# The last gates of an encoder trunk: two products moved ahead of a sum of squares, first outputs scaled on other engines, and squares summed by TensorE

## The chip, the cores and the metric

The kernel runs on one core of one Trainium2 chip. A core has five engines that run side by side, each through its own instructions in order: TensorE (PE in the profile; its weight loads are PEld), VectorE (DVE), ScalarE (ACT), GpSimd (POOL) and SyncE (SP), which issues transfers. The metric is the device time of one execution in microseconds (us), of which several runs were taken; one more execution was profiled.

## What is computed

Two requests of 512 and 256 tokens (768 in all, 1024 features) go through a trunk of two layers. Cut to the part that matters here, the end of the second layer and the last norm:

```
x = x + square(relu(h @ mlp_w_up)) @ mlp_w_down
gate = sigmoid(rms_norm(x, norm_ple) @ ple_w_gate)
x = x + (p @ ple_w_proj) * gate
y = rms_norm(x, final_norm)
# rms_norm(x, g) = x * rsqrt(mean(x * x over the 1024 features) + 1e-6) * g
```

## The kernel before, in words

Features lie on the partitions: x is 8 blocks of 128 features by 768 tokens, the first sequence's 512 tokens and then the second's 256. A product in near-fp32 accuracy is made of three: high weight by high input, high by low, low by high. So one gate product for one feature block is 8 x 3 = 24 matmuls into one PSUM bank. A sum over the features (over the partitions) is a matmul with a block of ones, whose result is the sum on every partition.

`last_ple` (line 1842) is the end of the program. Each of its two sequences has its own last norm (`first` and `second`, of the class `Last`). Its parts are these:

- For the first sequence, a loop over the 8 feature blocks: `gated` loads the operand `pr` (the finished product `p @ ple_w_proj`, line 1715), multiplies the gate product by the norm's factor (`gt`, VectorE, line 1718), takes the sigmoid (ScalarE, 1719), multiplies (VectorE, 1689) and adds to x (VectorE, 1721). `first.square` squares the new block (ScalarE, 257) and adds it to an accumulator (VectorE, 258).
- Then the code is laid out by hand: inside `tc.manual_schedule` the order on ScalarE, TensorE and VectorE is the order in which the code is written. The accumulator is split in two parts (`ah` on ScalarE, `al` on VectorE, both line 105/106), the second sequence's gate products 0 and 1 are made, and two matmuls with ones sum `ah` and `al` (the first sum of squares, tile `ss`). Out of it come a logarithm, an exponential, a square and three VectorE steps, lines 315 to 330; the result is the first sequence's factor `rf`.
- For the second sequence, block m by block m: `gate_of(m)` is the gate product, the load of its `pr` (line 1872) and the multiplication `gt` (1874); `sigmoid` (1879); `added` multiplies by `pr` (1689) and adds to x (1882); `shifted` squares the block on ScalarE (1886, 1888) and writes `y`, the block times its gain (1909). The squares of blocks 0 to 4 are added up on VectorE (1890). Between these stand the first sequence's outputs, `stored`: one VectorE instruction each that multiplies x by gain and by `rf` (1902), and a transfer out (1903).
- At the end four matmul terms in plain fp32 with ones (1960) sum the accumulator and the squares of blocks 5, 6 and 7; then come the same steps to a factor, the multiplication of `y` (1971) and four transfers out (1972).

SyncE issues the transfers in the order of the program. One whose data isn't there yet holds up those behind it.

Of the kernel before, what the change touches and what calls it, by code (L numbers as in the profile page):

```python
# [11 lines left out]
F32 = mybir.dt.float32  # L12
F32R = mybir.dt.float32r
AF = mybir.ActivationFunctionType
ALU = mybir.AluOpType
# [3 lines left out]
P = 128  # L19
D = 1024  # L20
KB = D // P
# [7 lines left out]
CH = 1024  # L29
# [19 lines left out]
def trunk_kernel(ctx: ExitStack, tc: tile.TileContext, a: dict, out: bass.AP):  # L49
    nc = tc.nc  # L50
    act, dve, pe = nc.scalar, nc.vector, nc.tensor
# [30 lines left out]
    def gain(i, m):  # L82
        return vec[:, i * KB + m : i * KB + m + 1]
# [10 lines left out]
    ones32 = const.tile([P, P], F32, name="ones32")  # L94
# [32 lines left out]
    def bank(tag, name):  # L127
        pool = pair_of_banks if tag == "B" else psum
        return pool.tile([P, 512], F32, tag=tag, name=name, bufs=BANKS[tag])

    def fresh(name="mm", n=1, tag=None):

        nonlocal shift
        if tag is None:
            shift += 1
            tag = "ACAB"[shift % 4]
        return bank(tag, name) if n == 1 else [bank(tag, name) for _ in range(n)]
# [62 lines left out]
    more = None  # L200

    def slot(i, name, dt=F32R, n=T):

        return (slots if i < 32 else more).tile([P, n], dt, tag=f"S{i}", name=name)

    def big(name, dt=F32):

        nonlocal turn
        if more is None:
            return tmp.tile([P, T], dt, tag="t", name=name)  # L210
        turn += 1
        return tmp.tile([P, T], dt, tag=f"q{turn % 6}", name=name, bufs=1)
# [733 lines left out]
    more = ctx.enter_context(tc.tile_pool(name="more", bufs=1))  # L946
# [6 lines left out]
    def x(m, o=0, n=T):  # L953
        return pairs[m // 2][:, m % 2, o : o + n]
# [737 lines left out]
    def gate(w, xs, o, n):  # L1692
        ts = terms_of(w, [[t[:, o : o + n] for t in p] for p in xs])
        if n == T:
            gp = both("gate")
            for j in range(2):
                for i, (wh, wl, xh, xl) in enumerate(ts):
                    for wt, xt in ((wl, xh),) if j else ((wh, xh), (wh, xl)):
                        for t, b, e in pieces(gp):
                            matmul(  # L1700
                                t,
                                wt,
                                xt[:, b:e],
                                start=i == j == 0 and xt is xh,
                                stop=i == len(ts) - 1 and j == 1,
                            )
            return pieces(gp)
        gp = fresh("gate")
        group(gp, ts, n)
        return [(gp[:, :n], 0, n)]  # L1710
# [131 lines left out]
    def last_ple(norm, ws, gps, parts, _, prs, ys, finals):  # L1842

        s0, s1 = SEQS
        first, second = Last(0, s0, *finals[0]), Last(s0, s1, *finals[1])

        def product(fin, m):
            return gate(ws[m], norm.xs, fin.o, fin.n)

        def block(fin, m, gp=None):  # L1850
            return gated(1, m, gp or product(fin, m), r, fin.o, fin.n, fin, prs)

        gps.append(product(first, 2))
        r = norm.rstd(psum, norm.sum_squares(psum, parts=parts))
        for m in range(KB):
            xb = block(first, m, gps[m] if m < 3 else None)
            if m < KB - 1:
                first.square(m, xb)

        groups = ((0, 1), (1, 2), (3, 3), (6, 2))  # L1860
        ys = [slot(i, "y", F32).rearrange("p (m n) -> p m n", n=s1) for i in ys]
        y = {m: ys[m // 3][:, m % 3, :] for m in range(KB)}

        outs = []
        left = list(range(KB))
        adds, held = [], []

        def gate_of(m):

            [(ps, _, _)] = product(second, m)  # L1870
            pr = slot(prs[m % 3], "pr", F32)
            nc.sync.dma_start(pr[:, :s1], pj[1][m, :, s0:])
            t = big("gt")
            dve.tensor_tensor(t[:, :s1], ps, r[:, s0:], ALU.mult)
            return t, pr

        def sigmoid(gate):
            t = gate[0]
            second.gated = act.activation(t[:, :s1], t[:, :s1], AF.Sigmoid).ins

        def added(m, t, pr):
            dve.tensor_tensor(x(m, s0, s1), x(m, s0, s1), gate_times(pr, t, s1), ALU.add)

        def squared(m):
            if m == 0:
                return act.activation(second.acc, x(m, s0, s1), AF.Square)
            sq = second.temp("sq")
            act.activation(sq, x(m, s0, s1), AF.Square)
            if m < KB - 3:
                adds.append(lambda: dve.tensor_tensor(second.acc, second.acc, sq, ALU.add))  # L1890
            else:
                held.append(sq)

        def stored(n):

            for _ in range(n):
                i = left.pop(0)
                if i % 2 == 0:
                    tag = ("sum0", "sum1", "zhi", "zlo")[i // 2]
                    outs.append(more.tile([P, CH], F32, tag=tag, name="o", bufs=1))  # L1900
                o = outs[i // 2][:, i % 2 * s0 : i % 2 * s0 + s0]
                dve.scalar_tensor_tensor(o, x(i, 0, s0), gain(6, i), rf, ALU.mult, ALU.mult)
                nc.sync.dma_start(out[i, :, :s0], o)

        ET = mybir.EngineType
        def shifted(m):
            if m < KB - 1:
                squared(m)
                act.activation(y[m], x(m, s0, s1), AF.Copy, scale=gain(6, m))

        with tc.manual_schedule(engines={ET.Activation, ET.PE, ET.DVE}):
            first.last = first.gated
            first.table()
            first.square(KB - 1, xb)
            parts = first.acc_parts()
            gates = [gate_of(m) for m in range(2)]
            ss = first.sum_squares(psum, parts=parts)
            logs, newton, result = first.rstd_steps(psum, ss)
            logs()
            newton()  # L1920
            result()
            rf = first.r
            for m in range(2):
                sigmoid(gates[m])
            added(0, *gates[0])
            shifted(0)
            gates.append(gate_of(2))
            sigmoid(gates[2])
            added(1, *gates[1])
            shifted(1)  # L1930
            for m in range(2, KB - 2):
                if m > 2:
                    gates.append(gate_of(m))
                    sigmoid(gates[m])
                for _ in range(len(adds)):
                    adds.pop(0)()
                if m > 2:
                    stored((2, 1, 2)[m - 3])
                added(m, *gates[m])
                if m < KB - 3:  # L1940
                    shifted(m)
            gates.append(gate_of(KB - 2))
            sigmoid(gates[KB - 2])
            shifted(KB - 3)
            t, pr = gates[KB - 2]
            pr = gate_times(pr, t, s1)
            gates.append(gate_of(KB - 1))
            sigmoid(gates[KB - 1])
            dve.tensor_tensor(x(KB - 2, s0, s1), x(KB - 2, s0, s1), pr, ALU.add)
            shifted(KB - 2)  # L1950
            added(KB - 1, *gates[KB - 1])
            m = KB - 1
            second.last = second.gated
            second.table()
            sq = second.temp("sq")
            dve.tensor_tensor(sq, x(m, s0, s1), x(m, s0, s1), ALU.mult)
            ss = fresh("ss")[:, :s1]
            terms = [second.acc, *held, sq]
            for i, z in enumerate(terms):
                pe.matmul(ss, lhsT=ones32[:], rhs=z, start=i == 0, stop=i == len(terms) - 1)  # L1960
            stored(1)
            logs, newton, result = second.rstd_steps(psum, [(ss, 0, s1)])
            logs()
            act.activation(y[m], x(m, s0, s1), AF.Copy, scale=gain(6, m))
            stored(2)
            newton()
            result()
            rf = second.r
            for m, n in groups:
                yb = ys[m // 3][:, m % 3 : m % 3 + n, :]  # L1970
                dve.tensor_tensor(yb, yb, rf[:, None, :].broadcast_to([P, n, s1]), ALU.mult)
                nc.sync.dma_start(out[m : m + n, :, s0:].rearrange("m p t -> p m t"), yb)
# [213 lines left out]
    held = old[8:13]  # L2186
# [124 lines left out]
```

## Time and profile before

| what | us |
|---|---|
| three runs: median (lowest to highest) | 1590.61 (1590.45 to 1590.7) |
| the profiled execution, its own time | 1591.22 |
| its span in the trace | 1589.4 |
| TensorE busy in the span | 1543.9 |
| last gate product of the first sequence ends | 1547.3 from the start |
| last matmul of the second sequence's gate products ends | 1576.3 from the start |

The profiled execution's time is 1.8 us more than its span. Times within the trace are counted from the span's start. A timeline row gives start, duration, engine, line, operation, tiles and a count, and in brackets how long the engine had stood idle and what ended that; "x18" are 18 merged instructions. A windows row gives a stretch, its length, the busy time of PE, PEld, DVE, ACT and POOL (with instruction counts), the clock granted to TensorE (1.00 is full), the DMA engines' busy share and GB/s.

### The profile page before, as it was taken

The page shows a single profiled execution, that of the slowest core. Times are in us where ns is not written, and L with a number is a line of the kernel's source. Part 1 is how long each engine was busy: PE and PEld are TensorE (multiplying, and loading weights), DVE is VectorE, ACT ScalarE, POOL GpSimd, SP SyncE. Part 2 cuts the span into 40 slices and gives each one's busy share as a digit, 9 for nine tenths or more (in the row PEclk, how much of TensorE's full clock was granted, in tenths as well). Part 3 has the DMA queues.
Part 4 walks back from the last instruction along what each step waited for, and adds up shares of the span by engine and source line. Part 5 has one row for each costly group of instructions (what it writes and reads, how often), then busy time and mean ns, then how long its engine had stood idle before and what let it go on. Part 6 is the DMA issues. An engine that isn't in the chain of part 4 may idle for free.

```text
span 1589.4 us, 24597 instructions
## 1 busy us (share of the span) xinstructions
PE 1543.9 (97%) x9375; PEld 1489.7 (94%) x9375; DVE 1357.7 (85%) x2244; ACT 982.2 (62%) x1566; POOL 151.0 (9%) x172
## 2 busy tenths in 40 slices
PE   9999999999999999999989999999999999999996
PEld 7988889999999999999989999999999999999885
DVE  7599898898889889889898887869888988988986
ACT  7478766876566656667755344556656665665754
POOL 0211000011111111110000000000111111111000
PEclk9999999999999999999999999999999999999998
DMA  8854412445654644556522212122564554456522
GB/s 278 216 135 134 132 52 91 128 100 129 137 120 120 140 115 105 129 137 152 147 60 80 80 67 85 63 78 69 138 137 114 128 139 102 108 137 140 138 78 103
DMA packets 72694, 188.39 MB, mean 119 GB/s; under 512 B 8144, under 2 KB 26064, under 8 KB 72576
## 3 DMA queue, kind: packets, MB, share of 16 engines
q1 hardware_dynamic: 45440, 139.89, 28.3%
q0 software_dynamic: 27136, 46.93, 16.7%
q8 instruction: 73, 1.20, 0.3%
q14 instruction: 45, 0.37, 0.1%
HBM read 143.02 MB, written 10.48 MB: 97 GB/s over the span
## 4 chain that ended last, share of the span: by engine, by line
PE 61%; DVE 22%; ACT 10%; issue 4%; DMA 4%; SPq 0%; DVEq 0%; ACTq 0%
PE a L180 28%; PE mm L180 7%; PE b L180 6%; PE B L180 4%; PE C L180 4%; PE c L180 3%; PE d L180 2%; DVE t L424 2%; PE pt L847 1%; ACT y L1149 1%; PE gate L180 1%; PE p L180 1%; DVE act L463 1%; DVE pr L1689 1%; PE O L857 1%
## 5 line engine op out<-in xcount | busy, mean ns | idle before, releaser
L180 PE MATMUL a<-xs,whi 128*128 128x384 f32 x624 | 116.0, 329 | 11.2 <-DVE y L1389 9.9
L180 PEld LDWEIGHTS a<-xs,whi 128*128 128x128 f32 x624 | 102.5, 189 | 16.4 <-DVE y L1389 13.8
L180 PE MATMUL a<-t,zhi 128*128 128x384 f32 x568 | 109.5, 326 | 0.0
L180 PE MATMUL a<-t,whi 128*128 128x384 f32 x568 | 109.3, 326 | 0.0
L180 PE MATMUL b<-t,zhi 128*128 128x384 f32 x552 | 106.7, 326 | 0.3 <-DVE t L424 0.3
L180 PE MATMUL a<-act,whi 128*128 128x384 f32 x512 | 104.3, 326 | 0.0
L1475 POOL DMA_DIRECT2D x<-p x56 | 68.0, 1215 | 367.2 <-DVE x L1457 216.0
L504 ACT ACTIVATE whi<-sum 128x1024 fp32r<-128x1024 f32 x71 | 74.9, 1055 | 41.9 <-PE a L180 39.1
L532 DVE TENSOR_TENSOR wlo<-wraw,whi 128x1024 fp32r<-128x1024 f32 x74 | 90.1, 1218 | 10.9 <-ACT whi L504 10.9
L180 PEld LDWEIGHTS a<-t,whi 128*128 128x128 f32 x568 | 94.9, 189 | 0.6 <-ACT d L1565 0.6
L180 PEld LDWEIGHTS a<-t,zhi 128*128 128x128 f32 x568 | 95.1, 189 | 0.4 <-DVE t L424 0.4
L180 PEld LDWEIGHTS b<-t,zhi 128*128 128x128 f32 x552 | 92.3, 189 | 0.9 <-DVE t L424 0.9
L504 ACT ACTIVATE vhi<-wraw 128x512 fp32r<-128x512 f32 x71 | 44.4, 625 | 75.3 <-PE B L180 64.3
L504 ACT ACTIVATE zhi<-sum 128x1024 fp32r<-128x1024 f32 x71 | 74.8, 1054 | 22.2 <-DVE sum L480 22.2
L532 DVE TENSOR_TENSOR wlo<-sum,whi 128x1024 fp32r<-128x1024 f32 x71 | 86.5, 1218 | 2.2 <-ACT whi L504 2.2
L1457 DVE TENSOR_TENSOR x<-x,a 128x384 f32<-128x384 f32 x128 | 67.3, 549 | 23.6 <-PE a L180 11.8
L180 PEld LDWEIGHTS a<-act,whi 128*128 128x128 f32 x512 | 86.6, 189 | 0.3
L532 DVE TENSOR_TENSOR zlo<-sum,zhi 128x1024 fp32r<-128x1024 f32 x69 | 84.0, 1217 | 0.0
L504 ACT ACTIVATE whi<-wraw 128x1024 fp32r<-128x1024 f32 x76 | 79.4, 1045 | 1.9
L180 PE MATMUL mm<-xs_mix,whi 128*128 128x512 f32 (+1 forms) x320 | 77.3, 331 | 0.4 <-DVE pjs L610 0.4
L418 ACT ACTIVATE t<-y 128x768 fp32r<-128x768 f32 x64 | 52.3, 838 | 22.9 <-DVE y L409 17.3
L1457 DVE TENSOR_TENSOR x<-x,C 128x384 f32<-128x384 f32 x64 | 35.1, 553 | 35.3 <-PE C L180 29.2
(336 smaller groups left out, 4424.7 us busy)
## 6 DMA issues: line engine op xcount, KB each, us to landing
wraw<-in_up SPq DMA_DIRECT2D x64, 512.0 KB, 4.8
wraw<-in_down SPq DMA_DIRECT2D x64, 512.0 KB, 4.9
x<-p POOLq DMA_DIRECT2D x56, 384.0 KB, 6.4
wraw<-in_w_in SPq DMA_DIRECT2D x24, 512.0 KB, 3.5
vlo<-in_down POOLq DMA_DIRECT2D x32, 256.0 KB, 7.5
wraw<-in_gate SPq DMA_DIRECT2D x16, 512.0 KB, 4.1
vlo<-in_up POOLq DMA_DIRECT2D x28, 256.0 KB, 7.3
pj<-pjs SPq DMA_DIRECT2D x16, 384.0 KB, 2.8
```

The lines of the kernel that those rows point to most:

```text
L180: pe.matmul(ps, lhsT=w, rhs=rhs, **flags)
L418: act.activation(t[0][:], (self.q1, self.q2)[i][:], AF.Copy)
L424: dve.tensor_tensor(lo[:], (self.q1, self.q2)[i][:], hi[:].bitcast(F32), ALU.subtract)
L463: dve.tensor_tensor(lo[:], self.q2[:], hi[:].bitcast(F32), ALU.subtract)
L504: act.activation(hi[:], src, AF.Copy)
L532: dve.tensor_tensor(lo[:], src, hi[:].bitcast(F32), ALU.subtract)
L847: pe.transpose(pt[:, h * P : (h + 1) * P], lg[h // 2][:, h % 2, b * P : (b + 1) * P], ident[:],)
L857: pe.matmul(O[:], lhsT=v, rhs=ph[:], start=b == 0, stop=False)
L1149: act.activation(t[:], t[:], AF.Square)
L1457: dve.tensor_tensor(t[:, o : o + H], t[:, o : o + H], f, op)
L1475: nc.gpsimd.dma_start(pairs[2 * h + 1][:, :, o : o + H], q, accum_op=ALU.add)
L1689: dve.tensor_tensor(q, q, natural(t[:, o:e]), ALU.mult)
```

## The change

Four things change in `last_ple`, and nothing elsewhere.

1. The second sequence's gate products 2 and 3 are made ahead of the first sum of squares (kept in `made`) instead of one by one afterwards.
2. The first outputs are made in two steps: ScalarE writes x times gain into the output tile (`scaled`, blocks 0 to 3 in the loop over the first sequence, 4 to 7 after the split of the accumulator), and GpSimd multiplies by `rf` in place. `stored` now asks for two outputs at a time, the first two before block 2 of the second sequence is added.
3. The second sequence's squares are not added on VectorE any more. Each is a matmul term into one PSUM tile `ss2`; `summed` issues the terms that have been gathered.
4. The four transfers of first outputs stand elsewhere among the loads of `pr`.

```
+        def scaled(i):
+            if i % 2 == 0:
+                tag = ("sum0", "sum1", "zhi", "zlo")[i // 2]
+                outs.append(more.tile([P, CH], F32, tag=tag, name="o", bufs=1))
+            o = outs[i // 2][:, i % 2 * s0 : i % 2 * s0 + s0]
+            act.activation(o, x(i, 0, s0), AF.Copy, scale=gain(6, i))
...
             if m < KB - 1:
                 first.square(m, xb)
+            if m < KB // 2:
+                scaled(m)
...
-            [(ps, _, _)] = product(second, m)
+            [(ps, _, _)] = made.pop(m) if m in made else product(second, m)
...
         def squared(m):
-            if m == 0:
-                return act.activation(second.acc, x(m, s0, s1), AF.Square)
-            sq = second.temp("sq")
+            sq = second.acc if m == 0 else second.temp("sq")
             act.activation(sq, x(m, s0, s1), AF.Square)
-            if m < KB - 3:
-                adds.append(lambda: dve.tensor_tensor(second.acc, second.acc, sq, ALU.add))
-            else:
-                held.append(sq)
+            held.append(sq)
+
+        def summed(last=False):
+            for sq in held:
+                pe.matmul(ss2, lhsT=ones32[:], rhs=sq, start=not counted, stop=last and sq is held[-1])
+                counted.append(sq)
+            held.clear()
...
                 o = outs[i // 2][:, i % 2 * s0 : i % 2 * s0 + s0]
-                dve.scalar_tensor_tensor(o, x(i, 0, s0), gain(6, i), rf, ALU.mult, ALU.mult)
+                nc.gpsimd.tensor_tensor(o, o, rf, ALU.mult)
                 nc.sync.dma_start(out[i, :, :s0], o)
...
             parts = first.acc_parts()
+            for i in range(KB // 2, KB):
+                scaled(i)
             gates = [gate_of(m) for m in range(2)]
+            made.update((m, product(second, m)) for m in (2, 3))
             ss = first.sum_squares(psum, parts=parts)
...
             rf = first.r
+            ss2 = fresh("ss")[:, :s1]
...
             shifted(1)
+            stored(2)
             for m in range(2, KB - 2):
                 if m > 2:
                     gates.append(gate_of(m))
                     sigmoid(gates[m])
-                for _ in range(len(adds)):
-                    adds.pop(0)()
+                if m > 3:
+                    summed()
                 if m > 2:
-                    stored((2, 1, 2)[m - 3])
+                    stored(2)
                 added(m, *gates[m])
                 if m < KB - 3:
                     shifted(m)
...
-            ss = fresh("ss")[:, :s1]
-            terms = [second.acc, *held, sq]
-            for i, z in enumerate(terms):
-                pe.matmul(ss, lhsT=ones32[:], rhs=z, start=i == 0, stop=i == len(terms) - 1)
-            stored(1)
+            held.append(sq)
+            summed(True)
+            ss = ss2
             logs, newton, result = second.rstd_steps(psum, [(ss, 0, s1)])
             logs()
             act.activation(y[m], x(m, s0, s1), AF.Copy, scale=gain(6, m))
-            stored(2)
             newton()
```

On TensorE, at the very end of the program, this is the order before: `gate_16561` is the second sequence's gate product 7, `ss_16600` its sum of squares.

```order
L180 MATMUL gate_16561<-xs_ple1_15896,gwr_15908 128x64x2x2
L180 MATMUL gate_16561<-xs_ple1_15895,gwr_15910 128x64x2x2
L1960 MATMUL ss_16600<-acc_final512_16033,ones32_126 128x256
L1960 MATMUL ss_16600<-sq_16557,ones32_126 128x256
L1960 MATMUL ss_16600<-sq_16592,ones32_126 128x256
L1960 MATMUL ss_16600<-sq_16598,ones32_126 128x256
```

All four terms stand behind the last gate product.

On TensorE of the changed kernel, in the middle of the second sequence: `gate_16464` is gate product 4, `gate_16507` is gate product 5, `ss_16424` is `ss2`, and its four inputs are the squares of blocks 0, 1, 2 and 3.

```order
L180 MATMUL gate_16464<-xs_ple1_15896,gwr_15907 128x64x2x2
L180 MATMUL gate_16464<-xs_ple1_15895,gwr_15909 128x64x2x2
L1904 MATMUL ss_16424<-acc_final512_16033,ones32_126 128x256
L1904 MATMUL ss_16424<-sq_16438,ones32_126 128x256
L1904 MATMUL ss_16424<-sq_16447,ones32_126 128x256
L1904 MATMUL ss_16424<-sq_16461,ones32_126 128x256
L180 MATMUL gate_16507<-xs_ple1_15782,gw_15959 128x64x2x2
```

Four terms of the sum now stand between gate products 4 and 5. The square of block 4 stands alone between products 5 and 6, those of 5, 6 and 7 behind product 7.

On SyncE, the transfers of the second sequence before: `pr` are the loads of the operand for gates 0 to 7 in order, `out<-o` the first sequence's outputs, 512 tokens each.

```order
L1872 DMA pr_16434<-pj1_134 128x256
L1872 DMA pr_16475<-pj1_134 128x256
L1872 DMA pr_16514<-pj1_134 128x256
L1903 DMA out<-o_16440 128x512 x2
L1872 DMA pr_16552<-pj1_134 128x256
L1903 DMA out<-o_16481 128x512
L1872 DMA pr_16586<-pj1_134 128x256
```

The first three of these rows are the loads for gates 3, 4 and 5; those for 0, 1 and 2 stand ahead of them.

And the same place in the changed kernel, where the first `pr` row is the last of the three loads for gates 0 to 2, and the last two are those for gates 6 and 7:

```order
L1884 DMA pr_16357<-pj1_134 128x256
L1916 DMA out<-o_16086 128x512 x2
L1884 DMA pr_16450<-pj1_134 128x256
L1916 DMA out<-o_16109 128x512 x2
L1884 DMA pr_16489<-pj1_134 128x256
L1916 DMA out<-o_16297 128x512 x2
L1884 DMA pr_16532<-pj1_134 128x256
L1916 DMA out<-o_16300 128x512 x2
L1884 DMA pr_16569<-pj1_134 128x256
L1884 DMA pr_16603<-pj1_134 128x256
```

The load for gate 3 has moved behind two outputs, that for gate 4 behind four, that for gate 5 behind six, and those for gates 6 and 7 behind all eight.

More of the change, by code (lines that the diff above doesn't have):

```diff
@@ L1851, in block @@
             return gated(1, m, gp or product(fin, m), r, fin.o, fin.n, fin, prs)
+        outs = []
+        def scaled(i):
[4 more added lines that the diff above has]
+            act.activation(o, x(i, 0, s0), AF.Copy, scale=gain(6, i))
         gps.append(product(first, 2))
@@ L1862, in last_ple @@
         y = {m: ys[m // 3][:, m % 3, :] for m in range(KB)}
-        outs = []
         left = list(range(KB))
-        adds, held = [], []
+        held = []
+        made = {}
         def gate_of(m):
-            [(ps, _, _)] = product(second, m)
+            [(ps, _, _)] = made.pop(m) if m in made else product(second, m)
             pr = slot(prs[m % 3], "pr", F32)
@@ L1884, in squared @@
         def squared(m):
-            if m == 0:
-                return act.activation(second.acc, x(m, s0, s1), AF.Square)
-            sq = second.temp("sq")
+            sq = second.acc if m == 0 else second.temp("sq")
             act.activation(sq, x(m, s0, s1), AF.Square)
-            if m < KB - 3:
-                adds.append(lambda: dve.tensor_tensor(second.acc, second.acc, sq, ALU.add))
-            else:
-                held.append(sq)
+            held.append(sq)
[4 more added lines that the diff above has]
+            held.clear()
+        counted = []
         def stored(n):
@@ L1897, in stored @@
                 i = left.pop(0)
-                if i % 2 == 0:
-                    tag = ("sum0", "sum1", "zhi", "zlo")[i // 2]
-                    outs.append(more.tile([P, CH], F32, tag=tag, name="o", bufs=1))
                 o = outs[i // 2][:, i % 2 * s0 : i % 2 * s0 + s0]
-                dve.scalar_tensor_tensor(o, x(i, 0, s0), gain(6, i), rf, ALU.mult, ALU.mult)
+                nc.gpsimd.tensor_tensor(o, o, rf, ALU.mult)
                 nc.sync.dma_start(out[i, :, :s0], o)
```

## The prediction

> **What bounds the kernel now.** I read the page first, then the windows of the last 40 us, the timeline of TensorE there, and the chain of waits behind it. The page says that TensorE has work almost throughout:
>
> ```profile
> span 1589.4 us, 24597 instructions
> PE 1543.9 (97%) x9375; PEld 1489.7 (94%) x9375; DVE 1357.7 (85%) x2244; ACT 982.2 (62%) x1566; POOL 151.0 (9%) x172
> ```
>
> So only the places where TensorE is idle or slow can be won. The change touches the last 50 us; there the windows show a hole, a slow stretch and a full one:
>
> ```profile
> 1552.60:1556.50 3.90, 0.05 (x1) 0.00 (x0) 2.19 (x3) 2.74 (x4) 0.00 (x0) 0.89 0.12 34
> 1556.50:1562.70 6.20, 6.17 (x26) 5.64 (x27) 4.18 (x8) 3.96 (x6) 0.00 (x0) 0.52 0.00 0
> 1562.70:1576.30 13.60, 13.60 (x123) 13.60 (x123) 11.62 (x26) 6.36 (x17) 0.00 (x0) 1.00 0.43 147
> ```
>
> The hole of 3.9 us lowers the granted clock (the number behind the five busy times) to half for the 6.2 us that follow. The timeline of TensorE, line by line:
>
> ```profile
> 1552.37 0.28 PE L180 MATMUL gate<-xs_ple,zlo 128*128 128x256 f32 x1
> 1556.53 0.79 PE L180 MATMUL ss<-ah,ones 128*128 128x512 f32 x1 [3.88 <-ACT ah L105]
> 1557.25 0.79 PE L180 MATMUL ss<-al,ones 128*128 128x512 f32 x1
> 1557.84 4.04 PE L180 MATMUL gate<-xs_ple,gw 128*128 128x256 f32 x18
> 1561.68 1.23 PE L180 MATMUL gate<-xs_ple,gwr 128*128 128x256 f32 x6
> 1562.74 2.17 PE L180 MATMUL gate<-xs_ple,gw 128*128 128x256 f32 x18
> 1564.75 0.83 PE L180 MATMUL gate<-xs_ple,gwr 128*128 128x256 f32 x6
> 1565.42 2.17 PE L180 MATMUL gate<-xs_ple,gw 128*128 128x256 f32 x18
> 1575.47 0.83 PE L180 MATMUL gate<-xs_ple,gwr 128*128 128x256 f32 x6
> 1576.14 0.60 PE L1960 MATMUL ss<-acc_final,ones 128*128 128x256 f32 x2
> 1576.58 0.59 PE L1960 MATMUL ss<-sq,ones 128*128 128x256 f32 x2
> ```
>
> One gate product takes 1565.42 - 1562.74 = 2.68 us at full clock. Its matmuls come every (1564.75 - 1562.74)/18 = 0.112 us, at half clock every (1561.68 - 1557.84)/18 = 0.213. A term of the fp32 sum of squares is two matmuls and takes 1576.58 - 1576.14 = 0.44 us. Behind the last gate product the chain of waits leaves TensorE:
>
> ```profile
> 1576.35 0.43 DVE gt L1874
> 1580.07 0.42 DVE v L317
> 1581.07 0.75 DVE o L1902
> 1581.82 0.34 DVE v L323
> 1582.65 0.42 DVE y L1971
> ```
>
> From the hole's end the end hangs on TensorE, and from 1576.35 on a serial tail of 6.3 us to the first `y`. An `o` lies on the chain in that tail.
>
> **Products 2 and 3 in the hole.** They start where the hole starts, at 1552.5, and take 2 x 2.68 = 5.36 us, so the hole and the slow stretch go: the two sums with ones start at 1557.85. Each has 512 columns, twice a gate matmul, so 0.22 us. With the 0.17 by which the last matmul of a group outlives its step (0.28 against 0.11), `ss` is there at 1558.5 instead of 1557.25 + 0.79 = 1558.04. The factor is 0.4 us late.
>
> ScalarE and VectorE in that stretch:
>
> ```profile
> 1555.85 0.63 ACT L105 ACTIVATE ah<-acc_final 128x512 fp32r<-128x512 f32 x1 [0.76 <-DVE acc_final L258]
> 1558.14 0.69 ACT L315 ACTIVATE ln<-ss,eps 128x512 f32<-128x512 f32 x1 [1.67 <-PE ss L180]
> 1561.47 0.72 ACT L1879 ACTIVATE gt<-gt 128x256 f32<-128x256 f32 x2
> 1569.25 0.42 ACT L1888 ACTIVATE sq<-x 128x256 f32<-128x256 f32 x1 [1.97 <-DVE x L1882]
> 1569.58 0.49 ACT L1909 ACTIVATE y<-x,vec 128x256 f32<-128x256 f32 x1
> 1560.92 0.69 DVE L330 SCALAR_TENSOR_TENSOR rstd_final<-v,y 128x512 f32<-128x512 f32 x1
> 1563.81 0.42 DVE L1882 TENSOR_TENSOR x<-x,pr 128x256 f32<-128x256 f32 x1
> 1565.12 0.49 DVE L1689 TENSOR_TENSOR pr<-pr,gt 128x256 f32<-128x256 f32 x1
> 1565.64 0.43 DVE L1882 TENSOR_TENSOR x<-x,pr 128x256 f32<-128x256 f32 x1
> ```
>
> **Outputs by ScalarE.** An instruction with a gain takes 0.49 at 256 tokens against 0.42 for the square; at 512 tokens I take 0.63 + 0.07 = 0.70, or 0.61 from start to start (they overlap by 0.09, as 1569.25 + 0.42 and 1569.58 do). Blocks 0 to 3 go into a loop where ScalarE has gaps. Blocks 4 to 7 take 4 x 0.61 = 2.45 us between `ah` and `ln`. If `ah` ends at 1556.48 as before, ScalarE is free at 1559.0, and `ln` is 0.85 us late instead of 0.4. The order of VectorE's additions also changes in that loop and may bring `ah` forward. I take 0.5 late, bounds 0.4 and 0.85. So the factor is ready at 1560.92 + 0.69 + 0.5 = 1562.1.
>
> **VectorE without additions and outputs.** The first three blocks then run: x of block 1 starts at 1563.81 + 0.5 = 1564.3; the `pr` of block 2, which waited for an addition before, follows at once (1564.7 instead of 1565.12 + 0.5), x of block 2 ends at 1565.6. Then ScalarE does its square, `y` and the sigmoid of block 3 (0.33 + 0.40 + 0.42 from starts and ends of such rows) up to 1566.8, VectorE `pr` and x (0.52 + 0.43) up to 1567.75, and ScalarE the square of block 3 up to 1568.2. That is 1.45 us earlier than before (1569.25 + 0.42 = 1569.67), if the operand for block 3 has landed at 1566.8.
>
> **Outputs by GpSimd.** The trace has no such multiplication on GpSimd. Its nearest rows, and those of the operand's load:
>
> ```profile
> masks.py:199 POOL TENSOR_SCALAR_AFFINE_SELECT ident<-ident 128x128 f32<-128x128 f32 x1 | 0.3, 288 | 0.1
> masks.py:197 POOL MEMSET ident<- 128x128 f32 x1 | 0.2, 205 | 0.3 <-POOLq L2299 0.3
> L2299 POOL MEMSET const-float32-0.0<- 128x1 f32 x1 | 0.1, 100 | 0.2 <-issue 0.2
> pr<-pj SPq DMA_DIRECT2D x8, 128.0 KB, 2.1
> L1903 SPq DMA_DIRECT2D out<-o x8: 332/333/338, 1567.7 to 1581.8; - x8
> ```
>
> Writing alone costs (205 - 100)/127 = 0.83 ns an element, reading one tensor and writing (288 - 100)/127 = 1.48. One more tensor read at the same step makes 2.1, so 512 elements take 1.2 us as an estimate. Bounds are 0.85 (no cost for the second tensor) and 2.0 (the two engines disturb each other; a rival below). At 1.2, two outputs are ready at 1562.1 + 2.4 = 1564.5, SyncE needs 0.33 to issue the second, so the load for gate 3 is issued at 1564.9 and lands 2.1 later, at 1567.0: 0.2 late. So the square of block 3 is ready at 1568.4. Every 0.1 us more adds 0.2. The other loads are wanted late enough, as the next part shows (at 1.2 the eighth output is ready at 1571.7, the load for gate 6 lands at 1574.2).
>
> **The new wait on TensorE.** This is the term that decides. Products run in order, and the order puts the four terms of squares 0 to 3 ahead of product 5. Product 4 ends at 1557.85 + 0.43 + 2.68 = 1561.0. Then TensorE has only terms of 0.44 us as the squares come, and waits for square 3 until 1568.45: 7.4 us with about 1.3 us of work in them. Queued behind it are products 5, 6 and 7; for them wait `gt` 5, 6 and 7 and the tail. From there on the sum of squares of block 3 (0.44), product 5 (2.68), the term of square 4 (0.44), products 6 and 7 (5.36) take 8.92 us at full clock: the last product's matmuls are issued at 1577.4 instead of 1576.14, 1.2 late.
>
> The clock is the question. Two windows of 3.4 us of the trace that bear on it, the first up to the drop, the second with the least work among those that kept the clock:
>
> ```profile
> 1552.25:1555.66 3.41, 0.40 (x4) 0.21 (x2) 2.04 (x3) 2.46 (x3) 0.00 (x0) 1.00 0.07 16
> 337.11:340.53 3.42, 1.83 (x12) 1.53 (x10) 3.39 (x6) 2.90 (x5) 0.00 (x0) 1.00 0.00 0
> ```
>
> 0.40 us of work in 3.41 (12%) lost the clock, 1.83 (54%) kept it. The new wait has 1.3 in 7.4, 18%, with at most 30% in any such stretch: between the two, nearer to the first. So I take the half clock. [...] Square 3's term then takes 0.88, to 1569.35; product 5 at 0.213 a matmul would end at 1574.45 if wholly slow, and with the clock back at 1573 at 1573.8 (17 slow matmuls and 7 at 0.112). The rest is 0.44 + 5.36: the last product is issued by 1579.6, 3.45 late. Bounds are 3.1 and 4.1.
>
> [...]
>
> **The tail.** The squares of 5 and 6 are ready before that of 7, so the last term ends as before relative to the last product. The two outputs between `v` L317 and `v` L323 go from VectorE: L323 then waits for ScalarE's square, which ended about 1580.95, instead of starting at 1581.75. That gives 0.75 us back (0.6 to 0.8). The transfers of `y` are unchanged, and the outputs' transfers are over by then.
>
> **Sum.** +3.45 - 0.75 = +2.7 us against the profiled execution's 1591.22, which stands 0.6 above the median of 1590.61; against the median 1593.3. Without the clock's loss +1.2 - 0.75 = +0.5, so 1591.1. About 0.2% (3.2 us) is what a measurement of this kernel can tell from no change; I count changes by it.
>
> **Rivals.**
>
> *The clock holds* through the wait, since the terms of the squares keep TensorE awake. [...] Against it: the 12% window, and the 0.52 of the stretch after it, which shows that work of 70% of a window did not bring the clock back at once. 1591.1.
>
> *GpSimd gates the operand loads* (slower than before beyond the bound). The place is SyncE's queue: gate 3's load behind two outputs, gates 6 and 7's behind eight. At 2.0 us an output, gate 3's load lands at 1562.1 + 4.0 + 0.4 + 2.1 = 1568.6, so square 3 and all behind it come 1.6 us later than in the forecast: +4.3, 1594.9. From 1.45 us on the sum passes 3.2. Above 2.06 the loads for gates 6 and 7 also come late (1562.1 + 8t + 0.4 + 2.1 against the `gt` of gate 7 at 1579.8 + 2(t - 1.2) less 0.5), and each 0.1 costs 0.8. For it: VectorE reads two tensors from SBUF in most instructions of that stretch, while GpSimd would read two more, and no row shows how they share. Against it: the estimate of 1.2. [...]
>
> *The products do not wait*, so that products 4 to 7 run on and only the vector work paces the end (faster). Then x of block 7 would be ready 2.4 us earlier than before and the tail gives 0.75: 1587.4. The order of the matmuls speaks against it, and the rows show no matmul ahead of an earlier one.
>
> **How the numbers follow.** The forecast (slow clock, GpSimd near 1.2) 0.55, the clock holds 0.25, GpSimd gates 0.16, no wait 0.04. Of the forecast's 0.55, where the clock comes back late or `ah` is not earlier the sum passes 3.2: about 0.16 of it. Slower by over 0.2%: 0.16 + 0.15 = 0.31; faster: 0.03; within: 0.66. The range goes from the clock-holds case with GpSimd at 0.85 (+0.3, 1590.9), less 0.15 for `ln` and the tail at their better bounds and 0.25 for the spread of the runs shown, 1590.5, to GpSimd at 2.0 with the clock back late, 1594.9 + 0.65, and 0.4 for a later `ah`: 1596.0.
>
> **What would show it.** In the changed profile: no hole at 1552.5 and full clock up to product 4; `ln` L315 at 1558.5 to 1559; a wait of TensorE for ScalarE's square, in pieces, between 1561 and 1568.5; a granted clock of half in product 5; eight GpSimd rows near 1.2 us; no `o` between the two `v` of the tail. I am wrong if product 5 starts before square 3, if the clock stays full, if GpSimd takes over 1.45 us an output, or if VectorE's rows grow longer beside it.

## The result, and the profile after

| | us |
|---|---|
| before, beside it on the same chip: median of 4 runs (lowest to highest) | 1590.65 (1590.45 to 1590.83) |
| changed: median of 4 runs | 1599.51 (1596.8 to 1600.49) |
| ratio, with its 95% interval | 1.0053 [1.0036, 1.007] |
| changed, the profiled execution: its own time, its span | 1600.18, 1598.4 |

The changed kernel is slower by half a per cent, more than three times the loss forecast. The windows of the changed kernel show the new shape of the last 50 us: the wait of TensorE up to the term of square 3 (first two rows), product 5 at half clock (third row), and full speed afterwards. The columns are those of before.

```profile
1561.20:1564.00 2.80, 0.00 (x0) 0.00 (x0) 2.42 (x4) 1.34 (x3) 1.90 (x2) 0.89 0.01 3
1564.00:1575.20 11.20, 4.30 (x8) 2.05 (x9) 9.37 (x10) 4.17 (x11) 9.26 (x7) 0.50 0.62 224
1575.20:1580.58 5.38, 5.38 (x27) 5.29 (x26) 0.92 (x2) 0.83 (x3) 0.00 (x0) 0.51 0.18 47
1580.58:1586.40 5.82, 5.82 (x53) 5.77 (x52) 2.27 (x5) 1.54 (x4) 0.00 (x0) 1.00 0.01 1
```

The old hole of 3.9 us is gone, but TensorE now stands still or nearly so from 1561.1 to 1575.2 (4.3 us of work in the 14). In those same 14 us GpSimd (the last of the five busy columns) works for 11.2 us and VectorE for 11.8. The timeline of TensorE in the changed kernel:

```profile
1552.40 2.17 PE L180 MATMUL gate<-xs_ple,gw 128*128 128x256 f32 x18
...
1560.23 0.83 PE L180 MATMUL gate<-xs_ple,gwr 128*128 128x256 f32 x6
1565.62 1.22 PE L1904 MATMUL ss<-acc_final,ones 128*128 128x256 f32 x2 [4.55 <-ACT acc_final L1898]
1568.58 1.22 PE L1904 MATMUL ss<-sq,ones 128*128 128x256 f32 x2 [1.74 <-ACT sq L1898]
1571.47 1.22 PE L1904 MATMUL ss<-sq,ones 128*128 128x256 f32 x2 [1.67 <-ACT sq L1898]
1574.56 1.22 PE L1904 MATMUL ss<-sq,ones 128*128 128x256 f32 x2 [1.87 <-ACT sq L1898]
1575.22 4.40 PE L180 MATMUL gate<-xs_ple,gw 128*128 128x256 f32 x18
1585.70 0.83 PE L180 MATMUL gate<-xs_ple,gwr 128*128 128x256 f32 x6
```

The four terms come 2.9 to 3.1 us apart, each for ScalarE's next square. Product 5 starts only after the fourth. The wait is the one that was forecast, but the last term comes at 1574.56 instead of 1568.45. Who made the squares late is seen on VectorE. The timeline of VectorE in the changed kernel, from the first factor on:

```profile
1562.27 1.43 DVE L1689 TENSOR_TENSOR pr<-pr,gt 128x256 f32<-128x256 f32 x1 [0.31 <-ACT gt L1891]
1563.74 1.38 DVE L1894 TENSOR_TENSOR x<-x,pr 128x256 f32<-128x256 f32 x1
1565.04 0.41 DVE L1886 TENSOR_TENSOR gt<-gate,rstd_ple 128x256 f32<-128x256 f32 x1
1565.37 1.23 DVE L1689 TENSOR_TENSOR pr<-pr,gt 128x256 f32<-128x256 f32 x1
1566.64 1.38 DVE L1894 TENSOR_TENSOR x<-x,pr 128x256 f32<-128x256 f32 x1
1567.94 1.55 DVE L1689 TENSOR_TENSOR pr<-pr,gt 128x256 f32<-128x256 f32 x1
...
1572.15 1.45 DVE L1689 TENSOR_TENSOR pr<-pr,gt 128x256 f32<-128x256 f32 x1 [0.92 <-ACT gt L1891]
1573.63 0.42 DVE L1894 TENSOR_TENSOR x<-x,pr 128x256 f32<-128x256 f32 x1
```

And the eight multiplications on GpSimd, as its timeline merges them, and the first of them alone:

```profile
1562.10 11.16 POOL L1915 TENSOR_TENSOR o<-o,rstd_final 128x512 f32<-128x512 f32 x8 [59.71 <-DVE rstd_final L330]
1562.10 1.26 POOL L1915 TENSOR_TENSOR o<-o,rstd_final 128x512 f32<-128x512 f32 x1 [59.71 <-DVE rstd_final L330]
```

A `pr` or an x took 0.42 to 0.51 us before; here it takes 1.23 to 1.55 as long as GpSimd multiplies, which is until 1562.10 + 11.16 = 1573.26, and 0.42 for the row that starts after that. The 0.41 of `gt` in between did not change (0.42 before): it reads one operand from PSUM and one from SBUF, whereas `pr` and x read both from SBUF.

The ends of the rows tell more than their lengths. GpSimd's eight multiplications end at 1563.4, 1564.8, 1566.2, 1567.7, 1569.1, 1570.6, 1572.0 and 1573.3. VectorE's seven long rows end at 1563.70, 1565.12, 1566.60, 1568.02, 1569.49, 1570.90 and 1573.60, so each ends 0.28 to 0.36 us behind the multiplication during which it started. That GpSimd is the cause is at this point still only a coincidence in time; the experiments test it.

For a comparison of profiles I take the time from the start of the second sequence's product 2 to the end of the span, since that start varies from profile to profile for reasons upstream (1550.6 to 1555.1 in the profiles of this study): 1598.4 - 1552.40 = 46.0 us after. In the kernel before, product 2 runs later, behind the hole; there I take the place where it could have started, one step behind the last matmul of product 1 (1552.37 + 0.11): 1589.4 - 1552.48 = 36.9.

### The profile page after: what moved, and what is told of

The parts are those of the page before. It is cut to its first block, busy times and chain, and to the rows that moved or that the text cites. A ratio compares the mean times of both kernels' runs of the same rounds, so it can differ in the third digit from the quotient of the medians.

```text
span 1598.4 us, 24619 instructions
## 1 busy us (share of the span) xinstructions
PE 1548.7 (97%) x9383; PEld 1493.0 (93%) x9383; DVE 1358.1 (85%) x2232; ACT 987.2 (62%) x1574; POOL 162.2 (10%) x180
## 4 chain that ended last, share of the span: by engine, by line
PE 66%; DVE 18%; ACT 8%; issue 4%; DMA 3%; SPq 1%; DVEq 0%; ACTq 0%; POOLq 0%
PE a L180 28%; PE mm L180 9%; PE b L180 6%; PE B L180 4%; PE C L180 4%; PE gate L180 4%; PE c L180 3%; PE d L180 2%; PE p L180 1%; PE pt L847 1%; DVE t L424 1%; ACT y L1149 1%; DVE pr L1689 1%; DVE act L463 1%; PE O L857 1%
```

## The experiments

The theory: while GpSimd multiplies two tensors in SBUF, VectorE's instructions with two operands in SBUF are held, and squares 0 to 3, on which TensorE waits by its new order, come late. The rivals: the new order alone is at fault, with the half clock; or GpSimd's slowness delays the loads queued behind its outputs on SyncE. The first five kernels below are edits of the changed one, the next two of the kernel before, and the last builds on the second. The first four ran in one batch, in which the kernel before had a median of 1590.95 (21 runs), the other four in a second on another chip, with 1589.89 (27 runs). Each ratio is against the kernel before of the same batch.

**No multiplication on GpSimd.** The outputs' transfers stay, the order stays.

```diff
-                nc.gpsimd.tensor_tensor(o, o, rf, ALU.mult)
```

> The changed kernel without GpSimd's eight multiplications; the first sequence's outputs leave without the factor, everything else as it was. If GpSimd holds up VectorE's instructions with two SBUF inputs (theory one), those rows fall from 1.2 to 1.55 us back to 0.42 to 0.50, the square of block 3 starts at about 1568 instead of 1574.1, product 5 is still slow, and the time is about 1593 (6.5 below the changed kernel). If TensorE's wait for the squares alone made the kernel late and the long VectorE rows were hidden behind it (theory two), the time stays above 1598.

Measured: 1595.02 (1594.72 to 1598.01), ratio 1.0027 [1.0015, 1.0039]; from product 2 on 39.8 us, 6.2 less than the changed kernel. VectorE's groups of this kernel between 1560.9 and 1573.6 us (the last two numbers ahead of the idle time are busy us and mean ns), and then the same groups of the changed kernel between 1562 and 1574:

```profile
L1689 DVE TENSOR_TENSOR pr<-pr,gt 128x256 f32<-128x256 f32 x5 | 2.4, 489 | 2.1 <-ACT gt L1891 2.1
L1894 DVE TENSOR_TENSOR x<-x,pr 128x256 f32<-128x256 f32 x5 | 2.1, 426 | 0.2
```

```profile
L1689 DVE TENSOR_TENSOR pr<-pr,gt 128x256 f32<-128x256 f32 x4 | 5.7, 1414 | 1.2 <-ACT gt L1891 1.2
L1894 DVE TENSOR_TENSOR x<-x,pr 128x256 f32<-128x256 f32 x4 | 4.6, 1140 | 0.1
```

With the multiplications out, and nothing else, the mean of `pr` falls from 1414 to 489 ns and that of x from 1140 to 426. So GpSimd's work is what holds VectorE. What is left is +2.9 us against before: the order with its clock, less what the rest of the change wins (two experiments below part the two). TensorE's rows of this kernel show that the half clock stays:

```profile
1564.60 1.22 PE L1904 MATMUL ss<-acc_final,ones 128*128 128x256 f32 x2 [2.66 <-ACT acc_final L1898]
...
1568.94 1.22 PE L1904 MATMUL ss<-sq,ones 128*128 128x256 f32 x2 [0.91 <-ACT sq L1898]
1569.60 4.40 PE L180 MATMUL gate<-xs_ple,gw 128*128 128x256 f32 x18
```

Each term still takes 1.22 us and product 5's first 18 matmuls 4.40 instead of 2.17. But square 3's term is there 6.5 us sooner, counted from product 2's start (15.67 us against 22.16).

**All terms last.** Each square gets a place of its own, and all eight terms stand behind product 7; GpSimd multiplies as in the changed kernel.

```diff
+        sqs = [wp.tile([P, CH], F32, name="wraw", bufs=3) for _ in range(2)]
+        def place(m):
+            return sqs[m // 4][:, m % 4 * s1 : m % 4 * s1 + s1]
...
-            sq = second.acc if m == 0 else second.temp("sq")
+            sq = second.acc if m == 0 else place(m)
...
-                if m > 3:
-                    summed()
...
```

> The changed kernel with all terms of the second sum of squares behind gate product 7 (each square in a place of its own), GpSimd's multiplications kept. Theory one: the VectorE rows stay at 1.2 to 1.55 us until GpSimd ends at about 1573.3, the square of block 3 stays at about 1574, but products 5 to 7 no longer wait for it; from there the gates go on at 2.1 us each, the square of block 7 comes at about 1581.4 instead of 1588.5, and the time is about 1592.5. If the lateness of VectorE alone set the end, and the order on TensorE cost nothing, the time stays above 1598.

Measured: 1594.37 (1593.12 to 1598.29), ratio 1.0021 [1.0012, 1.003]; from product 2 on 39.5 us. TensorE no longer waits between the products. The window of this kernel, and then TensorE's rows for the last six matmuls of product 7 and for the last terms:

```profile
1561.00:1570.00 9.00, 9.00 (x83) 9.00 (x83) 7.94 (x9) 4.49 (x10) 6.62 (x5) 1.00 0.29 105
```

```profile
1569.54 0.83 PE L180 MATMUL gate<-xs_ple,gwr 128*128 128x256 f32 x6
1580.83 3.67 PE L1909 MATMUL ss<-wraw,ones 128*128 128x256 f32 x6 [1.55 <-ACT wraw L1903]
```

All products are done at 1570.4, which is 17.4 us earlier than in the changed kernel when both are counted from product 2's start, and at full clock, and still the kernel is slower than before: the last terms wait for squares, and VectorE's groups between 1560.9 and 1573.6 us show it held by GpSimd as in the changed kernel.

```profile
L1689 DVE TENSOR_TENSOR pr<-pr,gt 128x256 f32<-128x256 f32 x4 | 5.8, 1440 | 1.2 <-ACT gt L1891 1.2
L1894 DVE TENSOR_TENSOR x<-x,pr 128x256 f32<-128x256 f32 x3 | 4.2, 1391 | 0.1
```

The means of 1440 and 1391 ns stand against 489 and 426 without the multiplications. Removing the new wait removes only part of the loss, so the order is not its sole cause.

**Both: no multiplication, terms last.** The two edits together.

> Both: GpSimd's multiplications left out (the first sequence's outputs leave without the factor) and all terms behind product 7. With both causes gone only the vector work paces the end: block 7's square at about 1576 and the time about 1587.5, faster than the kernel before by 3. If a third cause is left (a late operand load, the late first factor), the time is above 1590.

Measured: 1587.33 (1585.8 to 1589.78), ratio 0.9978 [0.9968, 0.9987]; from product 2 on 32.9 us. VectorE's `pr` rows between 1560.9 and 1573.6 us are short, as without the multiplications alone:

```profile
L1689 DVE TENSOR_TENSOR pr<-pr,gt 128x256 f32<-128x256 f32 x6 | 3.0, 495 | 2.9 <-ACT gt L1891 2.9
```

The four corners, in us from product 2 to the end (before: 36.9):

| | GpSimd multiplies | left out | difference |
|---|---|---|---|
| terms ahead of product 5 | 46.0 | 39.8 | 6.2 |
| all terms last | 39.5 | 32.9 | 6.6 |
| difference | 6.5 | 6.9 | |

In the profiles the two costs add up almost exactly, and each is about the same with and without the other. The rest of the change wins 36.9 - 32.9 = 4.0 us. The medians of the runs have both costs too, but add up less well (4.5 and 7.0 us across, 5.1 and 7.7 down); the changed kernel has only four runs, 3.7 us apart, in a batch of its own.

**The wait filled.** Idle matmuls (`fill`, their results are overwritten) stand ahead of each of the first four terms, so that TensorE is busy through its wait.

```diff
-                if m > 3:
-                    summed()
+                if m == 4:
+                    bank5 = fresh("gate")
+                    for some in held[:4]:
+                        fill(18 if counted else 30)
+                        summed_one(some)
+                    held.clear()
+                elif m > 4:
+                    summed()
...
```

> The changed kernel with idle matmuls (30, then 18 each, results overwritten) ahead of the four terms between products 4 and 5, so that TensorE is busy for over four fifths of its wait. If the half clock is a cause of its own, the granted clock stays full, product 5 takes 2.7 us instead of 5.4 and a term 0.44 instead of 0.66 to 0.88, and the time falls by about 2.7 to 1597; the VectorE rows stay long. If the clock does not matter, 1599.5 as before.

Measured: 1597.91 (1597.27 to 1598.92), ratio 1.0044 [1.0029, 1.0059]; from product 2 on 43.4 us, 2.6 less than the changed kernel. Its window over the wait, and TensorE's rows at its end:

```profile
1561.80:1576.00 14.20, 12.63 (x94) 11.64 (x93) 12.30 (x13) 5.51 (x14) 11.33 (x8) 1.00 0.50 176
```

```profile
1575.67 0.70 PE L1923 MATMUL ss<-sq,ones 128*128 128x256 f32 x2 [0.29 <-ACT sq L1909]
1576.02 2.36 PE L180 MATMUL gate<-xs_ple,gw 128*128 128x256 f32 x18
```

The clock stays at 1.00 and product 5 starts at full speed, 2.36 us for 18 matmuls, so the half clock costs the changed kernel 2.6 us in the profiles. The medians give 1599.51 - 1597.91 = 1.6, and the two intervals overlap, so the size rests on the profiles' rows, not on the runs. The order without its clock is worth the rest, 43.4 - 39.5 = 3.9 us, or rather more: the kernel with all terms last loses its clock later, in the last terms (the 3.67 us for six matmuls above, 1.22 a pair, as in the changed kernel where 0.50 was granted), and takes 6.0 us from its last `gt` to its first `y` where the changed kernel takes 5.5.

**GpSimd with one tensor.** The multiplication takes the factor of one column instead of the whole tensor, so GpSimd reads one tensor.

```diff
-                nc.gpsimd.tensor_tensor(o, o, rf, ALU.mult)
+                nc.gpsimd.tensor_scalar(o, o, rf[:, 0:1], None, ALU.mult)
```

> The changed kernel with GpSimd's two-tensor multiplication replaced by one that reads a single tensor and a column of the factor (so the first sequence's outputs get one token's factor for all). If GpSimd holds up VectorE by its second tensor only, the VectorE rows with two SBUF inputs fall to 0.42 to 0.50 and the time is that of the run without multiplications, about 1595. If any GpSimd work on SBUF holds VectorE's two-input instructions, each of those rows still lasts about one GpSimd row (0.8 to 0.9 us), and the time lies between, about 1597.

Measured: 1594.73 (1593.44 to 1595.64), ratio 1.003 [1.0019, 1.0041]; from product 2 on 40.8 us. GpSimd did not get faster, but slower, 1650 ns an output against 1428 in the changed kernel. The group of this kernel on GpSimd:

```profile
L1915 POOL TENSOR_SCALAR o<-o,rstd_final 128x512 f32<-128x512 f32 x8 | 13.1, 1650 | 59.7 <-DVE rstd_final L330 59.7
```

VectorE's two groups between 1560.9 and 1573.6 us, and then single rows from its timeline, all in this kernel:

```profile
L1689 DVE TENSOR_TENSOR pr<-pr,gt 128x256 f32<-128x256 f32 x5 | 3.2, 648 | 3.6 <-DMA pr<-pj 3.3 <-ACT gt L1891 0.3
L1894 DVE TENSOR_TENSOR x<-x,pr 128x256 f32<-128x256 f32 x5 | 2.5, 502 | 0.2
```

```profile
1562.64 0.88 DVE L1689 TENSOR_TENSOR pr<-pr,gt 128x256 f32<-128x256 f32 x1
...
1564.41 0.81 DVE L1894 TENSOR_TENSOR x<-x,pr 128x256 f32<-128x256 f32 x1
...
1566.85 0.49 DVE L1689 TENSOR_TENSOR pr<-pr,gt 128x256 f32<-128x256 f32 x1 [1.30 <-DMA pr<-pj]
...
1570.16 0.50 DVE L1689 TENSOR_TENSOR pr<-pr,gt 128x256 f32<-128x256 f32 x1 [2.03 <-DMA pr<-pj]
```

The hold is much weaker: of the ten rows of the two groups three took 0.81 to 0.89, the rest 0.42 to 0.50, though GpSimd was at work throughout. Neither alternative came out whole: seven rows and the time are those of the first, three rows those of the second. So it matters what GpSimd does, not only that it works; that its second tensor read is what holds VectorE fits both kernels, but the two differ in the instruction too. In exchange the effect of the second rival, the queued loads, appears: at 1.65 us an output the loads of `pr` queued on SyncE behind the outputs (eight transfers, in pairs) do come late, and VectorE waits 1.30 and 2.03 us for them. In the changed kernel's same stretch VectorE waits for ScalarE alone.

**Products 2 and 3 alone**, on the kernel before.

```diff
+            made.update((m, product(second, m)) for m in (2, 3))
...
-            [(ps, _, _)] = product(second, m)
+            [(ps, _, _)] = made.pop(m) if m in made else product(second, m)
```

> The kernel before with only the two products moved ahead of the first sum of squares. If the loop of VectorE and ScalarE over the second sequence was as late as TensorE before, the last product is ready 7 us earlier and the time stays within 1 us of before (about +0.4 from the later factor). If TensorE's hole was what the end hung on, the time falls by 3 or more.

Measured: 1592.59 (1590.77 to 1594.58), ratio 1.0018 [1.0009, 1.0028]; from product 2 on 37.5 us, +0.6. The rows of TensorE and VectorE in this kernel:

```profile
1568.39 0.83 PE L180 MATMUL gate<-xs_ple,gwr 128*128 128x256 f32 x6
1573.08 0.67 PE L1962 MATMUL ss<-acc_final,ones 128*128 128x256 f32 x2 [3.85 <-DVE acc_final L1891]
1577.70 2.33 PE L1962 MATMUL ss<-sq,ones 128*128 128x256 f32 x4 [0.17 <-ACT sq L1889]
```

```profile
1576.39 0.42 DVE L1875 TENSOR_TENSOR gt<-gate,rstd_ple 128x256 f32<-128x256 f32 x1
```

The last product is done 7 us earlier, but the last `gt` stands at 1576.39, where it stood before (1576.35). The first factor comes 0.4 us later here (9.56 us against 9.13, counted as above), so in the kernel before VectorE and ScalarE were ahead of TensorE by about that, and no more. TensorE's lead of 7 us only turned into a wait and a half clock in the last terms (0.56 granted from 1573 to 1579): from the last `gt` to the first `y` it takes 6.8 us instead of 6.3. That is nearly all of the 0.6 us that the profile explains; the median is 2.7 above that of before, and where the other 2 us arise stays open: this one profile shows nothing of them between product 2 and the end.

**Outputs by ScalarE and GpSimd alone**, on the kernel before: `scaled` and `stored` as in the changed kernel, the order of products and the additions on VectorE as before.

```diff
...
-                dve.scalar_tensor_tensor(o, x(i, 0, s0), gain(6, i), rf, ALU.mult, ALU.mult)
+                nc.gpsimd.tensor_tensor(o, o, rf, ALU.mult)
...
```

> The kernel before with only the outputs moved to ScalarE and GpSimd. If GpSimd's instructions hold VectorE's, each of the eight 1.4 us slots lets one VectorE instruction with two SBUF inputs through; block 2 is added at about 1572 instead of 1566, and what VectorE saves later does not win it back: about 3 slower than before. If GpSimd works beside VectorE, the outputs leave VectorE's loop and the time falls by 1 to 2.

Measured: 1593.8 (1591.61 to 1596.3), ratio 1.0023 [1.0013, 1.0033]. From the end of the first factor to the end of the span, 30.8 us against 27.8 before: +3.0. Its groups on VectorE between 1562 and 1574.2 us:

```profile
L1689 DVE TENSOR_TENSOR pr<-pr,gt 128x256 f32<-128x256 f32 x4 | 4.7, 1182 | 0.3 <-ACT gt L1890 0.3
L1893 DVE TENSOR_TENSOR x<-x,pr 128x256 f32<-128x256 f32 x3 | 4.2, 1394 | 0.1
L1901 DVE TENSOR_TENSOR acc_final<-acc_final,sq 128x256 f32<-128x256 f32 x2 | 1.7, 874 | 0.8 <-ACT sq L1899 0.8
```

The same stretch of the kernel before, with its outputs:

```profile
L1902 DVE SCALAR_TENSOR_TENSOR o<-x,vec,rstd_final 128x512 f32<-128x512 f32 x5 | 3.6, 745 | 0.0
L1689 DVE TENSOR_TENSOR pr<-pr,gt 128x256 f32<-128x256 f32 x6 | 3.0, 493 | 0.3 <-ACT gt L1879 0.3
L1882 DVE TENSOR_TENSOR x<-x,pr 128x256 f32<-128x256 f32 x5 | 2.1, 425 | 0.2
L1890 DVE TENSOR_TENSOR acc_final<-acc_final,sq 128x256 f32<-128x256 f32 x4 | 1.7, 425 | 1.1 <-ACT sq L1888 1.0
```

The additions of squares are held as well, 874 ns against 425; they start later within a multiplication, and end 0.28 us behind it like the others. In this stretch five outputs are gone, 3.6 us, and the nine rows that remain are longer by 4 x 0.69 + 3 x 0.97 + 2 x 0.45 = 6.6 us. VectorE gets less done than before with its outputs on it. The hold needs neither the new order nor the half clock.

**A version from the findings.** All terms last, products 2 and 3 ahead as in the change, but the outputs on VectorE as before, placed one or two at a time where VectorE would wait.

```diff
-            if m < KB // 2:
-                scaled(m)
...
-                nc.gpsimd.tensor_tensor(o, o, rf, ALU.mult)
+                dve.scalar_tensor_tensor(o, x(i, 0, s0), gain(6, i), rf, ALU.mult, ALU.mult)
...
-                    stored(2)
+                    stored((1, 2, 1)[m - 3])
...
```

> Products 2 and 3 ahead, all terms of the second sum behind product 7, and the outputs by VectorE, one instruction each, in the gaps in which it waits for the sigmoid (1, 2 and 1 at gates 3 to 5, 1 each at gates 6 and 7, 2 in the tail). The run with neither cause was 4 us faster than before from product 2's start; about 1.3 us of the outputs do not fit into gaps, so 2.7 faster than before, about 1588. If VectorE is full without gaps, no faster than before.

Measured: 1588.22 (1586.74 to 1590.48), ratio 0.999 [0.9982, 0.9999]; from product 2 on 34.3 us, 2.6 less than before. Its rows on VectorE, an output and the `pr` behind it:

```profile
1563.86 0.74 DVE L1921 SCALAR_TENSOR_TENSOR o<-x,vec,rstd_final 128x512 f32<-128x512 f32 x1
1564.80 0.50 DVE L1689 TENSOR_TENSOR pr<-pr,gt 128x256 f32<-128x256 f32 x1 [0.20 <-ACT gt L1889]
```

Behind this single output VectorE still waits 0.20 us for ScalarE, so it fits where there was a wait anyway. Not all of them do: behind the pair at gate 4 no wait is left, and the kernel takes 1.4 us more than the one without any multiplications (32.9). This version beats both kernels, by a tenth of a per cent against the one before; its interval ends close to 1.

## Why the prediction was wrong, step by step

**Products 2 and 3 in the hole: right.** There is no hole, the clock is full up to product 4 (1.00 from 1555.5 to 1561.2), and product 4 ends at 1561.1 (1560.23 + 0.83), where 1561.0 was forecast. The factor was ready at 1562.0 (1561.27 + 0.69), where 1562.1 was forecast.

**VectorE without additions and outputs: this step failed.** It priced `pr` and x of blocks 0 to 3 as before, at 0.52 and 0.43 us, with nothing for GpSimd at work beside them, and put the square of block 3 at 1568.2 (1568.4 with the load). Seven of the eight rows took 1.23 to 1.55, and square 3's term came at 1574.56, 22.16 us after product 2's start instead of 15.95: 6.2 of the 6.4 us by which the sum was short. Without the multiplications the loss from product 2 on is +2.9, against a forecast of +2.7, and the parts agree as well: square 3's term at 15.67, the last product 3.6 late instead of 3.45, 0.8 won in the tail. So the rest of the sum was not right by luck.

**GpSimd at 1.2 us an output: mis-sized, which the failed step hid.** It took 1.43, within the bounds of 0.85 to 2.0 (the 2.0 was the author's estimate, no row shows it), and under the 1.45 from which that rival was to decide. Gate 3's load was issued at 1565.3, 0.4 later than forecast, and had landed long before VectorE came to it at 1572.15. Had VectorE been on time, it would have waited about 0.7 us for that load (landed at 1567.5, wanted at 1566.8); this is worked out from rows, no run shows it. The rival named the right neighbourhood, GpSimd and VectorE both reading two tensors from SBUF, but put its price on GpSimd's rows and on SyncE's queue. The bill came to VectorE. Only the last sentence of the text, VectorE's rows growing longer, said this, and it had no price. The rows show it: 0.42 to 0.51 became 1.23 to 1.55 us for the rows with two SBUF operands, and 0.41 stayed for the `gt` that reads PSUM.

**The new wait on TensorE: right.** Products 5 to 7 stood behind square 3's term. The experiments price it at 3.9 us without its clock beside GpSimd's work.

**The half clock: right.** Product 5 took 5.4 us instead of 2.68. The clock was back at 1580.6, 6.0 us after the last term started at 1574.56; the sum took 4.5, with the clock back at 1573, and this difference made the last product 0.65 us later. No run shows the 4.5, nor the bounds of 3.1 and 4.1 that stand beside the 3.45: in the kernel before, 6.1 us passed from the end of the hole to full clock (1556.5 to 1562.6), in the one without multiplications 5.5 from square 3's term (1568.94 to about 1574.4). The rival "the clock holds" is refuted: in the kernel without multiplications the longest gap was 2.66 us, where the changed kernel has one of 4.55, and yet its windows up to the drop and behind it look like this:

```profile
1560.80:1564.20 3.40, 1.14 (x11) 0.95 (x9) 2.40 (x5) 2.66 (x5) 0.00 (x0) 1.00 0.00 0
1564.20:1574.40 10.20, 8.86 (x29) 6.79 (x30) 4.47 (x11) 4.93 (x13) 0.00 (x0) 0.50 0.23 65
```

A stretch with 1.14 us of work in 3.40, a third, lost the clock.

**The tail: right.** No output stands in it. From the last `gt` to the first `y` it takes 5.5 us (1586.57 to 1592.06) instead of 6.3, so 0.8 was won where 0.75 was forecast. Another 0.4 came in the transfers behind.

**What the section on the bound left out.** It took TensorE alone to set the end from the hole on. Products 2 and 3 alone show that VectorE and ScalarE arrived only about 0.4 us ahead of it at the last `gt`. So there was next to nothing behind which a longer row on VectorE could hide.

## What to carry to other kernels

Before work is moved to an idle engine, price the neighbours' rows too, not only the engine's own: a row on VectorE that reads two SBUF tensors was lengthened threefold by a GpSimd instruction that does the same (`pr` from 489 ns without the multiplications to 1414 beside them), so eight outputs moved off VectorE cost it more than they had taken (6.6 us longer rows against 8 x 0.75 = 6.0, in the kernel with the outputs alone). Terms of a sum that wait for the vector engines belong behind the matmuls that don't, even where they look cheap (here 46.0 against 39.5 us from product 2 to the end). When a bound is read from the trace, look for the second engine that is just as late.

## What the runs showed of the hardware

- Beside GpSimd's two-tensor multiplication (128x512 fp32) in the changed kernel, VectorE's rows with two SBUF operands came at about the pace of GpSimd's instructions: from 1562.27 to 1566.64 VectorE started a held row after 1.47, 1.63 and 1.27 us, and GpSimd took 11.16 / 8 = 1.40 us each. Each held row ended 0.28 to 0.36 us behind the end of a multiplication. The rows with a PSUM operand kept their 0.41.
- The same multiplication with a column instead of a tensor took GpSimd longer (1650 ns against 1428), though it reads less, and lengthened only three of ten of VectorE's rows, to 0.81 to 0.89.
- In the kernel without multiplications TensorE's clock was lost with 1.14 us of work in 3.40 and no gap longer than 2.66 us. In the 10.20 us behind the drop 8.86 us of work, 87%, ran at 0.50.
